# A hybrid decoder block on one core: squares of the last token tile, a later norm, earlier loads for down, and the last sums

## The chip, the core and the metric

The kernel runs on one core of a Trainium2 chip. Its time is the device time of one execution in microseconds (us). The core has five engines with a queue of instructions each: TensorE (PE, with its weight loads PEld), VectorE (DVE), ScalarE (ACT), GpSimd (POOL) and SyncE (SP), which here only issues transfers. Each engine works its queue in order and waits for semaphores of the others.

## What is computed

One layer of a decoder block on 1024 tokens of width 1024: two groups of attention heads in parallel, an output projection, and a gated MLP of inner width 2816. Cut to the parts that the change touches:

```
x = x + concatenate([rmsnorm(nsa, nsa_norm_g), gdn]) @ w_out      # nsa: (tokens, 512)
h = rmsnorm(x, norm2_g)
x = x + (silu(h @ w_gate) * (h @ w_up)) @ w_down
return rmsnorm(x, final_g)

def rmsnorm(x, g):
    y = x * rsqrt(mean(x * x, axis=-1) + 1e-6)
    return y * g
```

## The kernel before

All large products keep fp32 accuracy by three products of a high and a low part: `split3` issues high by high (L119), high by low (L120) and low by high (L121). The parts are made by `split`: ACT writes the high part (a conversion, L1203), and POOL or VectorE subtracts it from the source (L1204). The instructions are written in program order; a scheduler with dependences places them in the queues, and `after(a, b)` holds TensorE's a behind b. Tiles live in rings of slots: a load waits until its slot's last reader is done.

Features lie on partitions and tokens along the free axis. Tokens go in two halves of 512, and features in tiles of 128 (dt 0 to 7).

*Norm of the sparse attention.* Per token tile i of 128 (NT of them), `nsa_square` (L1080) squares the attention output on ACT, and POOL adds its four feature tiles in two steps (L1083, L1084). `nsa_mean` (L1087) sums over partitions on TensorE with a column of ones (L1089); the tile's rows are then scaled (L1104), split into `mgt` (L1110 ACT, L1111) and multiplied by `w_out`.

*Second norm.* As each tile dt of the new x is there (L1176), `sumsq` squares it and adds it to `sqa` (L1195; for the last two of the second half on VectorE). `rnorm_sum` sums `sqa` over partitions on TensorE (L1212), VectorE scales it (L1215) and POOL takes the power -1/2 (L1216). `rnorm_out` spreads the result over partitions on TensorE (L1223). `normed` (L1361) multiplies x by it on VectorE, and `bsplit` (L1366) splits the result.

*MLP, up and gate.* Each of 22 blocks (256 columns of the gate for an even number, of the up for an odd one) is computed in Strassen's manner: products of 12 matmuls of operands A (weights, `Weights`, L1320) and B or T (activations). Block 0 is written out: `prod2` issues two products into one PSUM bank, 24 matmuls, and after step k of 8 (three matmuls each) calls what `between[k]` names. The first, `c11`, uses the first token half alone; the second half's norm is put between its matmuls, since its squares come last. Blocks 1 and 2 have two such products each. Then the loop over blocks (L1452) makes the seven-product sums on VectorE (L1466 to L1475), Silu for the gate on ACT (L1478), the gating product on POOL (L1481), and stores the gated tile in DRAM (`aD`, L1482), as SBUF doesn't hold all of them.

*Down.* `Pair(p)` (L1516) loads the weights of two inner tiles of 128 rows (`draw`, L1495, into the slots "wq" of the weights before) and their gated activations (`bact`, L1501, from `aD` into the ring of 20 slots); there are 11 pairs. Pair 0 is done as plain products (`lead`), pairs 1 to 9 in Strassen's manner, the last as plain products again (`trail`). `Plain` (L1541) splits the four weight tiles on VectorE and the four activation tiles on POOL. Slots for split tiles are handed out by `atile` (6 slots "A", 4 "wk").

*The end.* `trail` makes the last sum of x (L1634) for tokens 0 to 511, then 512 to 767, then 768 to 1023. ACT squares each tile (L1636), POOL adds dt 1 to 7, or 1 to 5 in the last part (L1640); `norm_sum` (L1608) sums over partitions (L1613), VectorE scales (L1616), POOL takes the power (L1617), `norm_out` spreads it (L1623). `scaled` (L1602) of the part before runs between, and stores to `out` (L1606); the last part's scaling is at L1658 to L1665.

## Time and profile before

| | before |
|---|---|
| median of 3 runs | 1481.53 us (1479.89 to 1483.02) |
| the profiled execution | 1479.02 us |
| its span in the profile | 1477.3 us |
| mean granted clock of TensorE | 0.990 |
| PE busy | 96% |
| PEld / DVE / ACT / POOL busy | 81% / 65% / 49% / 48% |
| chain that ended last | PE 61%, DVE 9%, issue 5%, POOL 5%, ACT 4%, DMA 3% |

The profile is of one execution, in us from the start of the span; about 1.7 us of the execution's time lie outside it. A row of the timeline names the start, the duration, the engine, the line of the kernel, the operation with output and input tiles, and how many in a row are drawn together; in brackets stands the idle time of the engine before it and what ended it. Matmuls overlap in the array, so one's duration is longer than the distance to the next. PEclk is the granted clock of TensorE as a share of 2.4 GHz; 0.50 is 1.2 GHz. The MLP's up and gate part runs from about 804 to 1240, down from there to 1465.

### The profile page before, as it was taken

How to read it: one execution, taken by the hardware profiler on the slowest of the kernel's cores; microseconds unless marked ns; L12 is line 12 of the kernel's file. 1: busy time of each engine (PE TensorE's matmuls, PEld its weight loads, DVE VectorE, ACT ScalarE, POOL GpSimd, SP SyncE). 2: the span in 40 equal slices, each digit the busy share in tenths (PEclk: the TensorE clock that was granted, in tenths of full speed). 3: DMA queues.
4: the chain of work that ended last, by engine and by line, in shares of the span. 5: the costliest groups of instructions: out<-in, count | busy, mean ns of one | idle time of the engine just before them, and what ended most of it. 6: DMA issues, size and time to landing. Idle time of an engine off the chain costs nothing.

```text
span 1477.3 us, 22838 instructions
## 1 busy us (share of the span) xinstructions
PE 1417.4 (96%) x7688; PEld 1194.4 (81%) x7688; DVE 965.9 (65%) x2270; ACT 717.6 (49%) x1568; POOL 715.0 (48%) x763
## 2 busy tenths in 40 slices
PE   8999999999998899999999999999999999999997
PEld 8998877999897777777777888888888887888886
DVE  4246688826645899999946954444444444999955
ACT  5433356336556988868754543333333331444423
POOL 1243235651122665654566186665566653345436
PEclk9999999999998999999999999999999999999998
DMA  7832255487536213110155132222222238534003
GB/s 273 275 113 74 96 173 165 115 214 223 160 124 213 82 51 108 50 44 23 43 180 191 29 115 93 83 79 74 79 85 80 86 98 286 190 117 135 1 1 114
DMA packets 142884, 174.92 MB, mean 118 GB/s; under 512 B 26928, under 2 KB 79408, under 8 KB 142640
## 3 DMA queue, kind: packets, MB, share of 16 engines
q1 hardware_dynamic: 142768, 173.47, 37.0%
q8 instruction: 61, 1.00, 0.3%
q14 instruction: 55, 0.45, 0.1%
HBM read 122.01 MB, written 51.41 MB: 117 GB/s over the span
## 4 chain that ended last, share of the span: by engine, by line
PE 61%; DVE 9%; issue 5%; POOL 5%; ACT 4%; DMA 3%; SPq 0%; POOLq 0%; DVEq 0%; ACTq 0%
PE mm L121 16%; PE mm L119 16%; PE mm L120 16%; PE c L1051 3%; PE b L1062 2%; DVE PT L1065 2%; PE a L1012 2%; PE a L650 1%; DVE cy L353 1%; ACT Ps L1029 1%; ACT PT L1064 1%; PE a L657 1%; POOL sqa L1640 1%; DMA mgt<-mgD 1%; PE a L964 1%
## 5 line engine op out<-in xcount | busy, mean ns | idle before, releaser
L1204 POOL TENSOR_TENSOR A<-wq,A 128x512 fp32r<-128x512 f32 x94 | 125.9, 1341 | 95.1 <-ACT A L1203 78.0
L1203 ACT ACTIVATE A<-wq 128x512 fp32r<-128x512 f32 x96 | 60.2, 631 | 134.4 <-PE mm L121 117.1
L119 PE MATMUL mm<-w,xh 128*128 128x256 f32 x384 | 110.6, 288 | 2.5 <-ACT kst L593 2.3
L120 PE MATMUL mm<-w,xh 128*128 128x256 f32 x384 | 110.0, 286 | 2.5 <-POOL w L208 2.5
L1065 DVE TENSOR_TENSOR PT<-b,PT 128x512 fp32r<-128x512 f32 (+1 forms) x148 | 100.9, 685 | 17.4 <-ACT PT L1064 16.6
L121 PE MATMUL mm<-w,xl 128*128 128x256 f32 x384 | 109.8, 286 | 0.0
L1204 POOL TENSOR_TENSOR wk<-wq,wk 128x512 fp32r<-128x512 f32 x61 | 82.4, 1352 | 55.2 <-ACT wk L1203 47.0
L1064 ACT ACTIVATE PT<-b 128x512 fp32r<-128x512 f32 (+1 forms) x148 | 86.1, 589 | 29.4 <-PE b L1062 27.7
L208 POOL TENSOR_TENSOR w<-wraw,w 128x512 fp32r<-128x512 f32 x48 | 64.0, 1353 | 57.7 <-ACT w L205 57.7
L1051 PE MATMUL c<-PT,vs 128*128 128x512 f32 x264 | 90.8, 430 | 0.1
L1203 ACT ACTIVATE wk<-wq 128x512 fp32r<-128x512 f32 x63 | 39.6, 630 | 87.7 <-PE mm L121 80.8
L119 PE MATMUL mm<-T,A 128*128 128x512 f32 x200 | 79.1, 396 | 0.0
L120 PE MATMUL mm<-T,A 128*128 128x512 f32 x200 | 79.1, 396 | 0.0
L121 PE MATMUL mm<-T,A 128*128 128x512 f32 x200 | 79.1, 396 | 0.0
L1481 POOL TENSOR_TENSOR ring<-ring,ring 128x512 f32<-128x512 f32 x44 | 58.4, 1327 | 38.9 <-DVE ring L1466 26.5
L119 PE MATMUL mm<-xh,w 128*128 128x512 f32 x192 | 76.0, 396 | 0.7 <-DVE kcl L417 0.7
L120 PEld LDWEIGHTS mm<-w,xh 128*128 128x128 f32 x384 | 73.5, 191 | 3.4 <-POOL w L208 3.3
L119 PEld LDWEIGHTS mm<-w,xh 128*128 128x128 f32 x384 | 73.5, 191 | 3.1 <-ACT kst L593 2.5
L121 PE MATMUL mm<-xh,w 128*128 128x512 f32 x192 | 75.3, 392 | 0.0
L120 PE MATMUL mm<-xl,w 128*128 128x512 f32 x192 | 74.8, 390 | 0.0
L1513 DVE TENSOR_TENSOR B<-B,mm 128x512 f32<-128x512 f32 x100 | 63.6, 678 | 16.1 <-PE mm L121 15.6
L121 PEld LDWEIGHTS mm<-w,xl 128*128 128x128 f32 x384 | 73.5, 191 | 0.1
(472 smaller groups left out, 4485.5 us busy)
## 6 DMA issues: line engine op xcount, KB each, us to landing
wq<-in_w_gu SPq DMA_DIRECT2D x92, 256.0 KB, 2.7
aD<-ring SPq DMA_DIRECT2D x44, 256.0 KB, 2.2
ring<-aD SPq DMA_DIRECT2D x44, 256.0 KB, 4.4
raw<-in_w_dn SPq DMA_DIRECT2D x36, 256.0 KB, 4.0
qk<-gD SPq DMA_DIRECT2D x16, 512.0 KB, 4.6
wraw<-in_w_out SPq DMA_DIRECT2D x28, 256.0 KB, 2.9
wraw<-in_w_tok SPq DMA_DIRECT2D x24, 256.0 KB, 2.9
wraw<-in_w_gdn SPq DMA_DIRECT2D x24, 256.0 KB, 2.9
```

Of the source, the lines that this page charges most:

```text
L119: after(mm(ps, lhsT=lh, rhs=rh, start=first, stop=False, skip_group_check=grow), prev)
L120: mm(ps, lhsT=lh, rhs=rl, start=False, stop=False, skip_group_check=grow)
L121: return mm(ps, lhsT=ll, rhs=rh, start=False, stop=last, skip_group_check=grow)
L208: (lo or G).tensor_tensor(out=wt[:, 1, k0:k0 + n, :], in0=raw, in1=f32(wt[:, 0, k0:k0 + n, :]), op=ALU.subtract)
L1012: mm(s1[:, 0:a1 - a0], lhsT=QS[:, h, :], rhs=KSs[a][:, g, a0:a1], start=(a == 0), stop=(a == 1))
L1051: mm(po, lhsT=v, rhs=PT[0:K, a], start=(n_ == 0 and a == 0), stop=(n_ == len(blocks) - 1 and a == 1))
L1064: act(out=PT[0:K, 0], in_=pt[0:K], func=AF.Copy)
L1065: V.tensor_tensor(out=PT[0:K, 1], in0=pt[0:K], in1=f32(PT[0:K, 0]), op=ALU.subtract)
L1203: act(out=dst[:, 0], in_=src, func=AF.Copy)
L1204: after(eng.tensor_tensor(out=dst[:, 1], in0=src, in1=f32(dst[:, 0]), op=ALU.subtract), prev)
L1481: G.tensor_tensor(out=t, in0=half[o], in1=t, op=ALU.mult)
L1513: V.tensor_tensor(out=out_, in0=a_, in1=b_, op=op)
```

## The change

It has four parts.

- A: for the last token tile the two POOL adds of the squares go, and `nsa_mean` sums the four parts in TensorE with four matmuls of 2 columns.
- B: in block 0 the sum of the second half's squares moves from behind step 2 of the first product to behind step 5, and the spreading of the norm from behind step 6 to behind step 1 of the second product `c21`.
- C: `draw`, `bact`, `lin` and `Pair` stand ahead of the block loop, and `Pair(0, True)` is made in the last block (b == NF - 1) behind `W.second()`, ahead of its products, instead of in `Plain`; so it is handed to `lead`.
- D: in the last part of the tokens, dt 4 and 5 too go to TensorE instead of POOL; the sums over partitions are ordered by part, with a PSUM bank for each 128 tokens; two VectorE operations scale them. The last scaled part is stored in four transfers of two tiles instead of two of four, by turns from SP's and from ACT's queue.

```
@@ -1080 @@ def nsa_square(i):
         act(out=sq, in_=mn[:, :, i * P:(i + 1) * P], func=AF.Square)
+        if i == NT - 1:
+            return sq
         G.tensor_tensor(out=sq[:, 0:2], in0=sq[:, 0:2], in1=sq[:, 2:4], op=ALU.add)
...
     def nsa_mean(i, sq, bank, tag, prev=None):
         pt = bank(tag)
-        after(mm(pt[:, 0:2], lhsT=sq[:, 0], rhs=ones[:, 0:2], start=True, stop=True), prev)
+        n = 4 if i == NT - 1 else 1
+        for k in range(n):
+            after(mm(pt[:, 0:2], lhsT=sq[:, k], rhs=ones[:, 0:2], start=k == 0, stop=k == n - 1), prev)
@@ -1407 @@
-    c11 = prod2(W.A11, B11, W.A12, B21, {2: norm1_sum, 6: norm1_out})
-    c21 = prod2(W.A21, B11, W.A22, B21)
+    c11 = prod2(W.A11, B11, W.A12, B21, {5: norm1_sum})
+    c21 = prod2(W.A21, B11, W.A22, B21, {1: norm1_out})
@@ -1459 @@ the loop over blocks
             W = wts.pop(b)
             W.second()
+            if b == NF - 1:
+                raws0 = Pair(0, True)
             p1, p2 = P12.pop(b) if b in P12 else (prod(W.A11, B11)[0], prod(W.A12, B21)[0])
@@ -1541 @@ class Plain:
-        def __init__(self, p, engs):
+        def __init__(self, p, engs, raws=None):
             self.fs = [2 * p, 2 * p + 1]
-            raws = Pair(p, True)
+            raws = raws or Pair(p, True)
...
-    lead = Plain(0, (V, G))
+    lead = Plain(0, (V, G), raws0)
@@ -1608 @@
-    def norm_sum(parts, w, prev=None):
+    def norm_sum(parts, w, prev=None, pss=None):
         n = w // P
-        ps = mk(pps4, [P, 512], "n", F32, 2)
-        for j in range(n):
-            for q_, t in enumerate(parts):
-                after(mm(ps[:, 2 * j:2 * j + 2], lhsT=t[:, j * P:(j + 1) * P], rhs=ones[:, 0:2], start=q_ == 0,
+        ps = pss[0] if pss else mk(pps4, [P, 512], "n", F32, 2)
+        for q_, t in enumerate(parts):
+            for j in range(n):
+                o_ = pss[j][:, 0:2] if pss else ps[:, 2 * j:2 * j + 2]
+                after(mm(o_, lhsT=t[:, j * P:(j + 1) * P], rhs=ones[:, 0:2], start=q_ == 0,
                          stop=q_ == len(parts) - 1), prev)
         ms = mk(pc, [P, 2, 4], "ms4", F32, 2)
-        V.tensor_scalar(ms[:, 0, 0:n], ps[:, 0:2 * n:2], 1.0 / D, EPS, op0=ALU.mult, op1=ALU.add)
+        if pss:
+            for j in range(n):
+                V.tensor_scalar(ms[:, 0, j:j + 1], pss[j][:, 0:1], 1.0 / D, EPS, op0=ALU.mult, op1=ALU.add)
+        else:
+            V.tensor_scalar(ms[:, 0, 0:n], ps[:, 0:2 * n:2], 1.0 / D, EPS, op0=ALU.mult, op1=ALU.add)
...
-            if dt >= 6 and o:
+            if dt >= 4 and o:
                 parts.append(s_[:, :w])
...
-    ms = norm_sum(parts, w)
+    ms = norm_sum(parts, w, None, [mk(pps4, [P, 512], "mm", F32, 6) for _ in range(w // P)])
...
-        if dt % 4 == 3:
-            dma(out[:, dt - 3:dt + 1, hf * 512 + o:hf * 512 + o + w], x2[hf][:, dt - 3:dt + 1, o:o + w])
+        if dt % 2:
+            (dma if dt % 4 == 1 else nc.scalar.dma_start)(
+                out[:, dt - 1:dt + 1, hf * 512 + o:hf * 512 + o + w], x2[hf][:, dt - 1:dt + 1, o:o + w])
```

In the changed kernel the lines from L1083 on have other numbers: L1212 is L1216 there, L1223 is L1227, L1204 is L1208, L1481 is L1531, L1482 is L1532, draw's load L1498 is L1451, bact's L1503 is L1456, L1489 is L1539.

TensorE in block 0, around the sum of the second half's squares (`sqa`); A and wk are the split weights, B_1766 the first and B_1767 the second feature half of the activations. Before:

```order
L119 MATMUL mm_9517<-B_1766_9288,A_9332 128x512
L120 MATMUL mm_9517<-B_1766_9288,A_9332 128x512 [waits DVE_49]
L121 MATMUL mm_9517<-B_1766_9288,A_9332 128x512
L1212 MATMUL mm_9527<-ones_81,sqa_9229 128x2 [waits DVE_49]
L1212 MATMUL mm_9527<-ones_81,sqa_9229 128x2 x3
L119 MATMUL mm_9517<-B_1766_9288,A_9332 128x512
L120 MATMUL mm_9517<-B_1766_9288,A_9332 128x512
```
Changed:

```order
L119 MATMUL mm_9518<-B_1767_9290,wk_9336 128x512 [waits Activation_49]
L120 MATMUL mm_9518<-B_1767_9290,wk_9336 128x512 [waits DVE_49]
L121 MATMUL mm_9518<-B_1767_9290,wk_9336 128x512
L1216 MATMUL mm_9537<-ones_81,sqa_9230 128x2 [waits DVE_49]
L1216 MATMUL mm_9537<-ones_81,sqa_9230 128x2 x3
L119 MATMUL mm_9518<-B_1767_9290,wk_9336 128x512 [waits Activation_49]
L120 MATMUL mm_9518<-B_1767_9290,wk_9336 128x512
```
The sum stands behind three steps of the second operand pair now; 12 matmuls lie between it and the spreading of the norm before and after.

SP's queue at the last gating: loads of weights for down (wq from `in_w_dn`), loads of the residual (B from `x3D`), stores of gated tiles (to `aD`) and loads of gated tiles (from `aD`). Before:

```order
L1498 DMA wq_12734<-in_w_dn 128x512
L1498 DMA wq_14348<-in_w_dn 128x512
L1498 DMA wq_14350<-in_w_dn 128x512
L1498 DMA wq_14352<-in_w_dn 128x512
L1489 DMA B_2319_12722<-x3D_68 128x4x512 x2
L1482 DMA aD_69<-ring_12635 128x512
L1489 DMA B_2320_12723<-x3D_68 128x4x512 x2
L1482 DMA aD_69<-ring_12679 128x512
L1503 DMA ring_12736<-aD_69 128x512
L1482 DMA aD_69<-ring_12651 128x512
L1503 DMA ring_12738<-aD_69 128x512
L1503 DMA ring_12740<-aD_69 128x512
```
Changed:

```order
L1451 DMA wq_12614<-in_w_dn 128x512
L1451 DMA wq_14349<-in_w_dn 128x512
L1456 DMA ring_12616<-aD_69 128x512
L1456 DMA ring_12618<-aD_69 128x512
L1456 DMA ring_12620<-aD_69 128x512
L1456 DMA ring_12622<-aD_69 128x512
L1451 DMA wq_14351<-in_w_dn 128x512
L1451 DMA wq_14353<-in_w_dn 128x512
L1539 DMA B_2328_12740<-x3D_68 128x4x512 x2
L1532 DMA aD_69<-ring_12653 128x512
L1539 DMA B_2329_12741<-x3D_68 128x4x512 x2
L1532 DMA aD_69<-ring_12697 128x512
```
The first four loads of gated tiles move from behind two of the last four stores and the residual to directly behind the first five weight loads.

POOL at the same place: gating products (L1481, changed: L1531) and splits of the first pair's activations (from a ring tile by L1204, changed: L1208). Before:

```order
L1204 TENSOR_TENSOR A_12604<-wq_12575,A_12604 128x512
L1481 TENSOR_TENSOR ring_12635<-ring_12494,ring_12635 128x512
L1481 TENSOR_TENSOR ring_12679<-ring_12538,ring_12679 128x512
L1481 TENSOR_TENSOR ring_12651<-ring_12510,ring_12651 128x512
L1481 TENSOR_TENSOR ring_12633<-ring_12492,ring_12633 128x512
L1204 TENSOR_TENSOR wk_12751<-ring_12736,wk_12751 128x512
L1204 TENSOR_TENSOR A_12754<-ring_12740,A_12754 128x512
L1204 TENSOR_TENSOR A_12763<-ring_12738,A_12763 128x512
L1204 TENSOR_TENSOR wk_12766<-ring_12742,wk_12766 128x512
```
Changed:

```order
L1208 TENSOR_TENSOR A_12605<-wq_12576,A_12605 128x512
L1208 TENSOR_TENSOR wk_12752<-ring_12616,wk_12752 128x512
L1208 TENSOR_TENSOR A_12755<-ring_12620,A_12755 128x512
L1531 TENSOR_TENSOR ring_12653<-ring_12495,ring_12653 128x512
L1208 TENSOR_TENSOR A_12764<-ring_12618,A_12764 128x512
L1208 TENSOR_TENSOR wk_12767<-ring_12622,wk_12767 128x512
L1531 TENSOR_TENSOR ring_12697<-ring_12539,ring_12697 128x512
L1531 TENSOR_TENSOR ring_12669<-ring_12511,ring_12669 128x512
L1531 TENSOR_TENSOR ring_12651<-ring_12493,ring_12651 128x512
```
Two of the four splits move ahead of the last four gating products, and two behind the first of them.

## Rows read from the trace of the kernel before

**Rows 1.** the page: busy us (share of the span) and instructions of each engine
```profile
PE 1417.4 (96%) x7688; PEld 1194.4 (81%) x7688; DVE 965.9 (65%) x2270; ACT 717.6 (49%) x1568; POOL 715.0 (48%) x763
```

**Rows 2.** the timeline of TensorE, 770: start us, us, engine line op, [idle before]
```profile
770.13 0.38 PE L1089 MATMUL mm<-ones,wx 128*128 128x2 f32 x2 [1.41 <-POOL wx L1084]
```

**Rows 3.** the timeline of TensorE, first product of the MLP
```profile
803.90 0.39 PE L119 MATMUL mm<-B,A 128*128 128x512 f32 x1
...
805.73 0.39 PE L121 MATMUL mm<-B,A 128*128 128x512 f32 x1
807.61 1.05 PE L1212 MATMUL mm<-ones,sqa 128*128 128x2 f32 x8 [1.50 <-DVE sqa L1195]
...
812.94 1.06 PE L1223 MATMUL mm<-cst,ms 128*128 128x128 f32 x8
...
815.69 0.40 PE L121 MATMUL mm<-B,A 128*128 128x512 f32 x1
```

**Rows 4.** the timeline of VectorE and GpSimd in the same stretch
```profile
806.87 0.68 DVE L1195 TENSOR_TENSOR sqa<-sqa,wx 128x512 f32<-128x512 f32 x1
...
808.94 1.39 POOL L1216 TENSOR_TENSOR ms<-ms,cst 128x4 f32<-128x4 f32 x1 [5.81 <-DVE ms L1215]
...
814.04 2.06 DVE L1361 SCALAR_TENSOR_TENSOR ring<-ring,vec,mm 128x512 f32<-128x512 f32 x3 [4.58 <-PE mm L1223]
```

**Rows 5.** busy us, PE PEld DVE ACT POOL; PEclk, DMA share, GB/s
```profile
809.00:812.00 3.00, 3.00 (x9) 2.32 (x8) 0.46 (x1) 0.00 (x0) 3.00 (x3) 0.50 0.00 0
```

**Rows 6.** the timeline of TensorE, last gating to down
```profile
1239.59 0.40 PE L121 MATMUL mm<-B,A 128*128 128x512 f32 x1
1241.70 0.98 PE L119 MATMUL mm<-wk,wk 128*128 128x512 f32 x3 [1.72 <-ACT wk L1203]
...
1248.42 0.39 PE L119 MATMUL mm<-wk,A 128*128 128x512 f32 x1
```

**Rows 7.** the timeline of SP's queue and ACT, same place
```profile
1239.74 1.40 SPq L1503 DMA_DIRECT2D ring<-aD  x3
...
1241.02 0.63 ACT L1203 ACTIVATE wk<-ring 128x512 fp32r<-128x512 f32 x1 [17.12 <-DMA ring<-aD]
```

**Rows 8.** the timeline at the end, and one stretch's busy times
```profile
1465.82 0.38 PE L1613 MATMUL n<-ones,sqa 128*128 128x2 f32 x2 [0.72 <-POOL sqa L1640]
...
1466.06 0.40 ACT L1636 ACTIVATE gu<-B 128x256 f32<-128x256 f32 x1
...
1467.67 0.16 DVE L1616 TENSOR_SCALAR ms<-n 128x2 f32<-128x2 f32 x1 [1.06 <-PE n L1613]
...
1472.00:1474.00 2.00, 0.00 (x0) 0.00 (x0) 0.40 (x2) 0.00 (x0) 0.49 (x1) 0.50 1.03 335
```

**Rows 9.** the timeline of TensorE, the sums over the first token half
```profile
783.69 0.28 PE L1212 MATMUL mm<-ones,sqa 128*128 128x2 f32 x2
...
786.29 0.48 PE L119 MATMUL mm<-mgt,wk 128*128 128x512 f32 x1
```

**Rows 10.** the timeline at 775, and line 1111's group: ns min/median/max
```profile
775.84 3.94 DVE L1111 TENSOR_TENSOR mgt<-mn,mgt 128x128 fp32r<-128x128 f32 x4 [0.71 <-ACT mgt L1110]
...
777.05 0.50 PE L120 MATMUL mm<-mgt,wk 128*128 128x512 f32 x1 [0.46 <-DVE mgt L1111]
...
L1111 DVE TENSOR_TENSOR mgt<-mn,mgt x4: 279/1262/1369, 775.8 to 779.5; 128x128 fp32r<-128x128 f32 x4
```

**Rows 11.** the timeline of GpSimd and TensorE in block 2
```profile
853.38 2.54 POOL L1204 TENSOR_TENSOR wk<-wq,wk 128x512 fp32r<-128x512 f32 x2
...
856.42 0.40 PE L121 MATMUL mm<-T,wk 128*128 128x512 f32 x1
```

**Rows 12.** SP's queue and VectorE around the last gating, and a stretch
```profile
1206.33 13.18 SPq L1498 DMA_DIRECT2D wq<-in_w_dn  x6
...
1242.20 1.70 DVE L1204 TENSOR_TENSOR wk<-wq,wk 128x512 fp32r<-128x512 f32 x1 [1.49 <-ACT wk L1203]
...
1260.00:1280.00 20.00, 20.00 (x89) 16.39 (x88) 20.00 (x30) 6.57 (x12) 6.52 (x4) 1.00 0.45 167
```

More of the change, by code (lines that the diff above doesn't have):

```diff
@@ L1439, in hybrid_block, with draw, bact, lin @@
         bsplit(T4, k, h0b, V)
+    NRAW, NAB = 16, 8
+    def draw(src, early):
+        r = flat(mk(praw, [P, 4, P], "wq", F32, RAWB)) if early else mk(pm, [P, 512], "raw", F32, NRAW)
+        if src is not None:
+            dma(r, src)
+        return r
+    def bact(f, hf):
+        r = ring()
+        dma(r, aD[f, hf])
+        return r
+    def lin(out_, a_, b_, op):
+        V.tensor_tensor(out=out_, in0=a_, in1=b_, op=op)
+        return out_
+    ADD, SUB = ALU.add, ALU.subtract
+    class Pair:
+        def __init__(self, p, early):
+            self.early = early
+            self.a = {(d, c): draw(w_dn[:, 2 * p + c, d * 512:(d + 1) * 512], early) for c in range(2) for d in range(2)}
+            self.b = {(c, h): bact(2 * p + c, h) for c in range(2) for h in range(2)}
+            self.s1 = draw(None, early)
+        def operands(self, m):
+            a, b = self.a, self.b
+            if m == 1:
+                return a[0, 0], b[0, 0]
+            if m == 5:
+                return lin(self.s1, a[1, 0], a[1, 1], ADD), lin(b[0, 0], b[0, 1], b[0, 0], SUB)
+            if m == 6:
+                lin(a[1, 0], a[0, 0], a[1, 0], SUB)
+                return lin(a[0, 0], self.s1, a[0, 0], SUB), lin(b[0, 0], b[1, 1], b[0, 0], SUB)
+            if m == 3:
+                return lin(self.s1, a[0, 1], a[0, 0], SUB), b[1, 1]
+            if m == 7:
+                return a[1, 0], lin(b[0, 1], b[1, 1], b[0, 1], SUB)
+            if m == 2:
+                return a[0, 1], b[1, 0]
+            return a[1, 1], lin(b[1, 0], b[1, 0], b[0, 0], SUB)
     half = {}
@@ L1489, in hybrid_block @@
             dma(x2[hf][:, 4 * a:4 * a + 4], x3D[hf, 4 * a:4 * a + 4].rearrange("k p t -> p k t"))
-    def draw(src, early):
-        r = flat(mk(praw, [P, 4, P], "wq", F32, RAWB)) if early else mk(pm, [P, 512], "raw", F32, NRAW)
-        if src is not None:
-            dma(r, src)
-        return r
-    def bact(f, hf):
-        r = ring()
-        dma(r, aD[f, hf])
-        return r
     def dsplit(src, eng, early=False):
```

27 lines of the change are left out of this document (removed).

## The prediction

> **What bounds the kernel now.** I read the busy shares of the page first: TensorE works 1417.4 us of a span of 1477.3 [rows 1], so only time in which TensorE stands still, or runs at its lower clock, can be won. I therefore went through TensorE's rows of the timeline for idle time in front of them, and looked for those of the four places that the change touches. They lie in different stages, and each is read there.
>
> - Last token tile's norm: TensorE is idle 1.41 us until the second of two POOL adds of the squares (L1083, L1084) ends [rows 2].
> - First product of the MLP: it starts at 803.90 and keeps 0.229 us per product matmul (eight steps to 805.73). The sum of squares could then start at 805.96 and starts at 807.61, since VectorE ends its last add only at 806.87 + 0.68 = 807.55 [rows 3, 4]. Behind that wait the granted clock is 0.50, the 1.2 GHz level, from 809 to 812 [rows 5].
> - First product of down: the last gating matmul starts at 1239.59, the next could follow at 1239.82, and comes at 1241.70; there ACT's conversion of a tile waited 17.12 us for its load [rows 6, 7].
> - The end: TensorE waits 0.72 us for POOL's last add of squares; then the transfers run at a DMA share of 1.03 [rows 8].
>
> The span is 1477.3 and the execution 1479.02. The sums are made against 1479.02; the median of the runs, 1481.53, is 2.5 above it, and I carry the same difference over.
>
> **A, the last token tile's squares.** Two POOL adds go, and TensorE sums four parts: 8 instructions instead of 2. Such instructions were issued 24 in 786.29 - 783.69 = 2.60 us, 0.108 each [rows 9], so six more cost 0.65. TensorE wins 1.41 - 0.65 = 0.76 there. What is late next is the first product with this tile. Its ACT conversion (L1110, at 775.51) stands behind another conversion that a load feeds, and doesn't move; VectorE's four subtractions behind it take 3.94 us in all, and TensorE waits for three of them, 0.46 at the first [rows 10]; the others are 0.33 and 0.34. The shortest of the four takes 0.28, the median is 1.26 [rows 10], and in the timeline each long one ends as a POOL split ends. POOL loses 1.19 us of adds (0.74 and 0.45), but its next splits hang on ACT's conversions, and I find it only some 0.15 earlier. So nearly all is given back: **0.2 us**, between 0.1 and 0.76.
>
> The Trainium skill (GPSIMD Engine Reference, section Specifications) says that GpSimd's memory interfaces are shared with VectorE, with contention where a VectorE instruction has two SBUF inputs. The rows above show that stretch; without such a rule the subtractions would take 0.28 each and A would be worth 0.7.
>
> **B, the second half's norm.** The sum goes from behind 9 matmuls to behind 18, the broadcast from behind 21 to behind 30; nothing is added. The 30th matmul's slot ended at 815.69 + 0.23 = 815.92. A small group costs its 1.05 or 1.06 less the 0.39 - 0.229 = 0.16 that matmuls overlap, so 0.89 and 0.90. With no wait and the full clock the same point comes at 803.90 + 30 x 0.229 + 0.89 + 0.90 = 812.56. That is **3.36 us**: 1.65 of waiting, and the 12 matmuls between sum and broadcast, which took 812.94 - 808.50 = 4.44 instead of 2.75, 1.69 [rows 3]. The cover: TensorE reaches the sum at 803.90 + 18 x 0.229 = 808.02, and VectorE is done at 807.55, a margin of 0.47. From the sum's end to the end of POOL's power it took 808.94 + 1.39 - 808.50 = 1.83 [rows 4], so the power is there at 808.91 + 1.83 = 810.74, and TensorE asks for it at 808.91 + 12 x 0.229 = 811.66. The operands of the nine matmuls that now come sooner were written before 804.4 (VectorE's adds of squares at 804.35 and 806.87 stand behind them).
>
> But the second half's normalization on VectorE hangs on the broadcast: it starts 1.10 behind it, at 814.04 [rows 4], and will start at 811.66 + 1.10 = 812.76, only 1.28 earlier, where TensorE is 3.36 earlier. The chain of VectorE, ACT and POOL that feeds the products loses 2.08 us of its lead. From 815 to 1239 TensorE has no idle time in the timeline; the smallest lead that I find is in block 2: POOL ends a split at 853.38 + 2.54 / 2 = 854.65, and TensorE wants it at 856.42 [rows 11], a lead of 1.77. It becomes -0.3, and with A's gain -0.5. So I take 3.36 - 0.5 = **2.8 us**; the bounds are 3.4 (nothing given back) and 1.6 (the chain isn't earlier at all, and the lead of 1.77 less A's gain is all there is).
>
> Of the granted clock the windows show 1.00 (2.4 GHz) up to 808 and 0.50 (1.2 GHz) from 809 to 812, after 1.65 us without a product and 0.89 of small matmuls. The wait of 1.41 of [rows 2] was followed by no such fall, nor were the 24 small matmuls of [rows 9] that had no wait ahead. With the wait gone I take the full clock. The Trainium skill (TensorE: Matmul & The Clock Gate, section HAM oscillation) says that a wait between bursts of matmuls is paid a second time, in throttled matmuls behind it. By it the 1.69 goes with the wait, as I take it; if the small group alone were the cause, 1.69 would stay.
>
> **C, the first pair of down.** Its four weight loads and four loads of activations are now asked for ahead of the last gating. In SP's queue the weights stand where they stood; four loads of activations go past two weight loads, the four loads of the residual and the stores of the last gated tiles, behind which they stood (1239.74 for three of them [rows 7]). The queue gives out that stretch's weight loads between 1206.33 and 1219.51 [rows 12], so the activations are asked for by 1220 at the latest and there by 1224 (the page's median for such a load is 4.4). The slots of their split tiles come free with the products of the last gating, by 1234.3 as I count them at 12 x 0.23 = 2.8 us for a product, so all eight splits can be done by about 1236, before TensorE wants them at 1239.82. TensorE needed until 1248.42 for the 24 matmuls that follow; from 1241.70 that is 6.72 against 24 x 0.229 = 5.50. Won: 1.88 + 1.22 = 3.10.
>
> What moves with them: one ACT conversion of an early activation now stands ahead of the last Silu and of the last gating's copy; of POOL's four splits two stand ahead of the last gating's four multiplications and two behind the first, whose stores so come up to 1 us later; these are read only at the end of down, so that costs nothing. Two splits of VectorE go from 1242 to before 1240, where VectorE waits for TensorE anyway; this cover matters, as VectorE is busy 20.00 of 20 us in 1260 to 1280 [rows 12] and must be 3 us earlier there. The two splits (1.70 [rows 12], and 1.42 for the other) give it just that. I take **3.0 us**, and 1.5 as the low end (half is given back by a VectorE that stays late).
>
> **D, the end.** Sums of dt 4 and 5 go from POOL to TensorE: 20 small instructions instead of 12, 8 x 0.108 = 0.86 more, that start with the last product at about 1465.1 instead of 1465.82. Sixteen take until 1466.8; the last four need ACT's square, done at 1466.06 + 0.40 [rows 8]; so TensorE is done at about 1467.3, and VectorE, which read the sums at 1467.67 [rows 8], can at 1467.4. It then has two short operations of 0.16 instead of one. The mean is there some 0.1 to 0.3 earlier. But the transfers take the DMA engines whole from 1470 to 1475.8 (share 1.03 in 1472 to 1474), and the finer outputs, half of them from ACT's queue, don't change the bytes. **0.1 us**, between -0.5 (no row shows a transfer from ACT's queue; two SP issues took 1.21) and 0.6. The Trainium skill (DMA: Bandwidth & Descriptors, section Rules for kernel authors) says that issuing from several engines doesn't help bandwidth and saves issue time alone. Going by that sentence D gets no more than 0.6, and the share of 1.03 agrees.
>
> **Sum:** 0.2 + 2.8 + 3.0 + 0.1 = 6.1. Execution 1472.9, median 1481.53 - 6.1 = **1475.4 us**.
>
> **Rivals.** *1. The feeders give most back.* Lead lost by B and a full VectorE in down keep TensorE waiting in block after block; B falls to 1.0 and C to 1.5: 2.5 in all, 1479.0. For it: VectorE at 20.00 of 20; against: the leads of the other blocks, 5 to 10 us. *2. The sum still waits or the clock falls anyway.* The margin is 0.47; if VectorE's add is 0.5 later, or the small group alone brings a clock of 0.50, B keeps 1.65 less the 0.5 given back: 1.15 and 3.3 from the rest, 4.45, so 1477.1. Against: the 24 small ones of [rows 9]. *3. Slower: ACT is blocked.* ACT works in order, and a conversion of the early activations now stands ahead of its last Silu and the copy of the last gating's product. If that load lands after 1232 instead of 1224, the copy, VectorE's adds and with them the PSUM banks stop, and TensorE stands until the load is there: as late as the old 1241.7, that is 9.7 us of waiting, less the 3.1 of C (down then follows without a wait) and the 3.1 of A, B and D: 3.5 us slower, 1485.0. It decides from the load's landing at 1232; against it stands the queue's last issue at 1219.5, 12 us before. *4. The loads stay where they were* (the pair's tiles come free too late): then C is 0 and the time 1478.4. The order of SP's queue speaks against it.
>
> **How the numbers follow.** Forecast 0.70, rival 1 0.12, rival 2 0.10, rival 3 0.05, rival 4 0.03. A measurement of this kernel can tell 0.2%, 3 us, from no change. Faster by more: forecast, rivals 2 and 4, 0.83; within: rival 1, 0.12; slower: rival 3, 0.05. The range: all highs are 0.76 + 3.4 + 3.1 + 0.6 = 7.9, which gives 1473.6, and 1.6 below for the runs' own spread (1479.89 against 1481.53), 1472.0; the upper end takes in rival 1 with some of that spread, 1480.0.
>
> **What would show it.** A: the idle 1.41 ahead of the tile's sum gone, the waits of the next tile's products longer by some 0.5. B: no wait ahead of the sum of squares, granted clock 1.00 throughout 803 to 816, the broadcast near 811.5, and a wait of under 1 us near 853. C: no idle time between the last gating and down, four loads asked for before 1220. D: the last sums ended by 0.3 sooner and a DMA share of 1 to the end. The forecast is wrong if a wait of over 1 us on ACT or VectorE appears in the last gating or in 1260 to 1320, or the clock shows 0.50 in the first products.

## The result

The changed kernel took 1475.04 us in the median (9 runs, 1471.59 to 1480.48) against 1482.14 before (9 runs). The ratio is 0.9949, with a 95% interval of 0.9936 to 0.9962: 7.6 us faster, between 5.6 and 9.5. 1475.4 was forecast. Timed again later, the same kernel stood at 0.9944 (0.9930 to 0.9958).

The page of the changed kernel: span, busy times and the chain that ended last.

```profile
span 1472.9 us, 22871 instructions
PE 1416.7 (96%) x7702; PEld 1196.2 (81%) x7702; DVE 963.6 (65%) x2271; ACT 717.6 (49%) x1568; POOL 723.9 (49%) x759
PE 62%; DVE 9%; issue 6%; POOL 4%; ACT 4%; DMA 2%; SPq 0%; DVEq 0%; POOLq 0%; ACTq 0%
```

TensorE's busy time is within 0.7 us of what it was [rows 1: 1417.4]; the span is 4.4 us shorter. That is less than the times say, and a span alone can't be read here. Up to 765 us both kernels issue the same instructions, and yet that stretch ended at 764.9 before and at 766.1 after; among the 14 traces of this study it ended between 764.9 and 768.3. So I compare stage by stage: I count the product matmuls (L119 to L121) back from the last one, and take the time between fixed ones. Both kernels have the same number of them.

| stage, by its start in the trace of before | before | after | difference |
|---|---|---|---|
| last token tile, 764.89 to 780.66 | 15.77 | 15.34 | -0.43 |
| second half's output products, to 802.75 | 22.09 | 21.95 | -0.14 |
| first products of the MLP, to 817.06 | 14.31 | 11.44 | -2.87 |
| blocks, to 1233.98 | 416.92 | 416.94 | 0.02 |
| last gating and first pair of down, to 1250.91 | 16.93 | 13.80 | -3.13 |
| down, to 1429.65 | 178.74 | 178.73 | -0.01 |
| down's end, to 1450.02 | 20.37 | 19.93 | -0.44 |
| last products, to 1464.82 | 14.80 | 16.55 | 1.75 |
| from the last product to the end of the span | 12.49 | 12.13 | -0.36 |

The sum is -5.61, after the last products gave 1.75 back. (The last row takes the spans to 0.01 us, 1477.31 and 1472.85.) The places, one after the other.

TensorE in the last token tile's stage (start us, us, engine, line, operation; in brackets the idle time before it and what ended it):

```profile
769.72 1.01 PE L1093 MATMUL mm<-ones,wx 128*128 128x2 f32 x8
...
776.91 0.51 PE L119 MATMUL mm<-mgt,wk 128*128 128x512 f32 x1 [0.32 <-ACT mgt L1114]
777.77 0.50 PE L120 MATMUL mm<-mgt,wk 128*128 128x512 f32 x1 [0.36 <-DVE mgt L1115]
```

The idle 1.41 of [rows 2] is gone, and eight small instructions stand in its place. But the first product with this tile now waits 0.32 for ACT's conversion, and the waits for VectorE's subtractions are still there, 0.36 for 0.46 [rows 10].

TensorE, VectorE and GpSimd (POOL) in the timeline around the first products:

```profile
804.48 0.39 PE L119 MATMUL mm<-B,A 128*128 128x512 f32 x1
...
808.99 1.05 PE L1216 MATMUL mm<-ones,sqa 128*128 128x2 f32 x8 [0.24 <-DVE sqa L1199]
...
812.74 1.05 PE L1227 MATMUL mm<-cst,ms 128*128 128x128 f32 x8
...
797.75 3.08 DVE L1370 TENSOR_TENSOR B<-ring,B 128x512 fp32r<-128x512 f32 x2
...
798.90 1.38 POOL L1199 TENSOR_TENSOR sqa<-sqa,wx 128x512 f32<-128x512 f32 x1 [0.33 <-ACT wx L1195]
...
808.25 0.69 DVE L1199 TENSOR_TENSOR sqa<-sqa,wx 128x512 f32<-128x512 f32 x1
...
813.83 2.07 DVE L1365 SCALAR_TENSOR_TENSOR ring<-ring,vec,mm 128x512 f32<-128x512 f32 x3 [3.49 <-PE mm L1227]
```

The busy times of a stretch there (PE, PEld, DVE, ACT, POOL; then the granted clock, DMA share, GB/s):

```profile
809.00:812.00 3.00, 3.00 (x17) 2.66 (x18) 1.30 (x3) 0.63 (x1) 1.58 (x2) 1.00 0.00 0
```

The clock is 1.00 where [rows 5] had 0.50. The sum still waits 0.24: VectorE ends its last add at 808.94, not 807.55 [rows 4], and TensorE comes at 808.59. Two splits of VectorE at 797.75 took 3.08 us where the same two took 1.97 before:

```profile
797.02 1.97 DVE L1366 TENSOR_TENSOR B<-ring,B 128x512 fp32r<-128x512 f32 x2
...
798.47 1.68 POOL L1195 TENSOR_TENSOR sqa<-sqa,wx 128x512 f32<-128x512 f32 x1 [0.62 <-ACT wx L1191]
```

The difference lies in the second of the two, 0.68 us before (from 798.32) and 1.78 after (from 799.05), and it goes with who starts first. Before, this split started 0.15 us ahead of GpSimd's addition of squares (798.47), and the addition took 1.68. After, it started 0.15 behind that addition (798.90), which took 1.38. All fourteen traces of this study go one way or the other: 0.68 us and ahead in the seven without part A, 1.78 us and behind in the seven with it. The normalization behind the broadcast starts at 813.83, only 0.21 earlier than in [rows 4].

POOL's split and TensorE's first use of its low part in block 2:

```profile
852.69 1.29 POOL L1208 TENSOR_TENSOR wk<-wq,wk 128x512 fp32r<-128x512 f32 x1
...
854.16 0.40 PE L121 MATMUL mm<-T,wk 128*128 128x512 f32 x1
```

The split ends at 853.98 and is wanted at 854.16: the lead was 1.77 [rows 11] and is 0.18, and TensorE doesn't wait.

SP's queue, POOL and TensorE at the last gating, and the stretch of [rows 12]:

```profile
1212.36 1.85 SPq L1456 DMA_DIRECT2D ring<-aD  x4
...
1232.91 1.29 POOL L1208 TENSOR_TENSOR wk<-ring,wk 128x512 fp32r<-128x512 f32 x1 [1.51 <-ACT wk L1207]
...
1237.32 0.40 PE L121 MATMUL mm<-B,A 128*128 128x512 f32 x1
1237.56 0.39 PE L119 MATMUL mm<-wk,wk 128*128 128x512 f32 x1
```

The busy times of a stretch there (PE, PEld, DVE, ACT, POOL; then the granted clock, DMA share, GB/s):

```profile
1260.00:1280.00 20.00, 20.00 (x89) 16.33 (x88) 20.00 (x31) 8.91 (x16) 8.40 (x5) 1.00 0.30 102
```

The four loads are asked for from 1212.36, the last split is done at 1234.20, and down's first product follows the gating at the distance of matmuls, 0.24. VectorE is still busy 20.00 of 20 us and holds nobody up.

TensorE at the first sum over partitions of the last products, and the clock behind it:

```profile
1446.96 1.05 PE L1622 MATMUL n<-ones,sqa 128*128 128x2 f32 x8 [1.06 <-POOL sqa L1653]
```

The same sum in the trace of before:

```profile
1452.55 1.05 PE L1613 MATMUL n<-ones,sqa 128*128 128x2 f32 x8 [0.81 <-POOL sqa L1640]
```

The busy times of a stretch behind it in the changed kernel (PE, PEld, DVE, ACT, POOL; then the granted clock, DMA share, GB/s):

```profile
1448.00:1450.00 2.00, 2.00 (x12) 2.00 (x12) 0.58 (x2) 0.28 (x1) 1.71 (x2) 0.57 0.00 0
```

This wait was 0.81 before, with a clock of 1.00 throughout; it is 1.06 here, and the clock fell to 0.57 in the mean of 1448 to 1450. That is the 1.75 given back.

The end: TensorE's small matmuls, VectorE's two scalings, the spreading, and the last transfers by SP and ACT:

```profile
1460.85 0.50 PE L1622 MATMUL mm<-ones,sqa 128*128 128x2 f32 x4
...
1463.02 0.31 DVE L1627 TENSOR_SCALAR ms<-mm 128x1 f32<-128x1 f32 x2 [0.50 <-PE mm L1622]
...
1464.17 0.71 PE L1636 MATMUL n<-cst,ms 128*128 128x128 f32 x4 [1.03 <-POOL ms L1630]
...
1466.49 1.22 SPq L1678 DMA_DIRECT2D out<-B  x2
1466.94 1.16 ACTq L1678 DMA_DIRECT2D out<-B  x2
```

The busy times of a stretch there (PE, PEld, DVE, ACT, POOL; then the granted clock, DMA share, GB/s):

```profile
1469.00:1471.00 2.00, 0.00 (x0) 0.00 (x0) 0.00 (x0) 0.00 (x0) 0.00 (x0) 0.50 1.04 344
```

From the last product matmul the sums are read 2.3 us later (1460.73 to 1463.02) instead of 2.9 (1464.82 to 1467.67, [rows 8]); the transfers run at a share of 1.04 up to the end, as before.

### The profile page after: what moved, and what is told of

It is laid out like the page before. It is cut to its first block, busy times and chain, and to the rows that moved or that the text cites. A ratio compares the mean times of both kernels' runs of the same rounds, so it can differ in the third digit from the quotient of the medians.

```text
span 1472.9 us, 22871 instructions
## 1 busy us (share of the span) xinstructions
PE 1416.7 (96%) x7702; PEld 1196.2 (81%) x7702; DVE 963.6 (65%) x2271; ACT 717.6 (49%) x1568; POOL 723.9 (49%) x759
## 4 chain that ended last, share of the span: by engine, by line
PE 62%; DVE 9%; issue 6%; POOL 4%; ACT 4%; DMA 2%; SPq 0%; DVEq 0%; POOLq 0%; ACTq 0%
PE mm L119 17%; PE mm L121 17%; PE mm L120 17%; PE c L1051 3%; PE b L1062 2%; DVE PT L1065 2%; PE a L1012 2%; PE a L650 1%; DVE cy L353 1%; ACT Ps L1029 1%; ACT PT L1064 1%; PE a L657 1%; DMA mgt<-mgD 1%; POOL sqa L1653 1%; PE a L964 1%
## 5 line engine op out<-in xcount | busy, mean ns | idle before, releaser
L1208 POOL TENSOR_TENSOR A<-wq,A 128x512 fp32r<-128x512 f32 x94 | 141.4, 1507 | 94.9 <-ACT A L1207 83.6
L119 PE MATMUL mm<-w,xh 128*128 128x256 f32 x384 | 111.2, 290 | 2.6 <-ACT kst L593 2.6
L121 PE MATMUL mm<-w,xl 128*128 128x256 f32 x384 | 110.5, 288 | 0.0
L1208 POOL TENSOR_TENSOR wk<-wq,wk 128x512 fp32r<-128x512 f32 x61 | 82.5, 1353 | 49.5 <-ACT wk L1207 44.8
L119 PE MATMUL mm<-T,A 128*128 128x512 f32 x200 | 79.1, 396 | 0.0
L121 PE MATMUL mm<-T,A 128*128 128x512 f32 x200 | 79.1, 396 | 0.0
L119 PEld LDWEIGHTS mm<-w,xh 128*128 128x128 f32 x384 | 74.2, 193 | 2.9 <-ACT kst L593 2.8
L119 PE MATMUL mm<-xh,w 128*128 128x512 f32 x192 | 75.9, 395 | 0.7 <-DVE kcl L417 0.7
L121 PE MATMUL mm<-xh,w 128*128 128x512 f32 x192 | 75.3, 392 | 0.0
L121 PEld LDWEIGHTS mm<-w,xl 128*128 128x128 f32 x384 | 74.3, 193 | 0.1
L353 DVE SCALAR_TENSOR_TENSOR cy<-cr,vec,cy 128x512 f32<-128x512 f32 x72 | 62.4, 867 | 17.1 <-ACT cy L351 7.3
```

The source lines that it names most:

```text
L119: after(mm(ps, lhsT=lh, rhs=rh, start=first, stop=False, skip_group_check=grow), prev)
L121: return mm(ps, lhsT=ll, rhs=rh, start=False, stop=last, skip_group_check=grow)
L353: V.scalar_tensor_tensor(out=y, in0=cr[:, j:j + 512], scalar=cw[:, j:j + 1], in1=y, op0=ALU.mult, op1=ALU.add)
L1208: after(eng.tensor_tensor(out=dst[:, 1], in0=src, in1=f32(dst[:, 0]), op=ALU.subtract), prev)
```

## The experiments

**Each part alone.** Four kernels, each the kernel before with one part of the change.

Part A:

```
+        if i == NT - 1:
+            return sq
...
-        after(mm(pt[:, 0:2], lhsT=sq[:, 0], rhs=ones[:, 0:2], start=True, stop=True), prev)
+        n = 4 if i == NT - 1 else 1
+        for k in range(n):
+            after(mm(pt[:, 0:2], lhsT=sq[:, k], rhs=ones[:, 0:2], start=k == 0, stop=k == n - 1), prev)
```

> Part A alone. By the ledger of the two traces A wins 0.95 us where the idle time ahead of the tile's sum was, and gives 0.5 back where VectorE's four subtractions end with POOL's splits: 0.4 us faster in all, ratio 0.9997, not to be told from 1 in the times, but plain in the trace as the distance from the last product before the sum to the first product of the second token half at 803.90. Rival: nothing holds those subtractions but their source, then the full 0.75 to 0.95 stays. Other rival: the first use of the tile hangs on loads and everything is given back, 0.

Measured: 1485.24 us, ratio 1.0022 (1.0011 to 1.0034): 3.3 us slower. TensorE at the tile's first product and at the sum of the second half's squares, and ACT's conversion ahead of the tile's:

```profile
777.71 0.50 PE L119 MATMUL mm<-mgt,wk 128*128 128x512 f32 x1 [1.10 <-ACT mgt L1114]
...
809.65 1.05 PE L1216 MATMUL mm<-ones,sqa 128*128 128x2 f32 x8 [2.21 <-DVE sqa L1199]
...
775.00 0.63 ACT L1207 ACTIVATE A<-wq 128x512 fp32r<-128x512 f32 x1 [1.75 <-DMA wq<-in_w_gu]
```

The 0.95 us won at the tile's sum (2.05 us from the product ahead of it to the one behind it became 1.10) are lost at once: the tile's conversion stands behind one that waited 1.75 us for its load, and TensorE waits 1.10 for it; the stage takes 15.94 us, 0.17 more than before. Then the sum of squares waits 2.21 instead of 1.50, and the first products take 15.06 instead of 14.31. None of the three had foreseen a loss. The traces account for 0.9 us of it, and 0.3 more in the first pair of down; 2 us of the 3.3 by the times are not seen in this one trace, which is that of the fastest of twelve runs (1481.41 us). Over the twelve, the mean granted clock was 0.987, against 0.989 in this trace and 0.988 over the 62 runs of the kernel before; so time at the lower clock is a likely place for the rest, not a shown one.

Part B:

```
-    c11 = prod2(W.A11, B11, W.A12, B21, {2: norm1_sum, 6: norm1_out})
-    c21 = prod2(W.A21, B11, W.A22, B21)
+    c11 = prod2(W.A11, B11, W.A12, B21, {5: norm1_sum})
+    c21 = prod2(W.A21, B11, W.A22, B21, {1: norm1_out})
```

> Part B alone. Theory: the wait ahead of the sum and the low clock behind it go together; 2.8 to 3.4 us, ratio 0.9977 to 0.9981, granted clock 1.00 from 804 to 816, and at most 0.4 us of idle time ahead of the sum. Rival 1: the group of eight small matmuls brings the clock down by itself; then 0.50 shows again behind it and 1.2 to 1.7 us are won, ratio 0.9989. Rival 2: the lead of the feeders in block 2 (1.77 us before) is used up: a wait of 0.3 to 1.0 us shows near 853, and 2.3 are won.

Measured: 1479.25 us, ratio 0.9981 (0.9969 to 0.9993). TensorE at the sum of squares (no idle time in front), then at the first pair of down, and the clock there:

```profile
810.03 0.95 PE L1212 MATMUL mm<-ones,sqa 128*128 128x2 f32 x8
...
1240.06 0.97 PE L119 MATMUL mm<-wk,wk 128*128 128x512 f32 x3 [1.41 <-ACT wk L1203]
1242.53 0.79 PE L120 MATMUL mm<-wk,wk 128*128 128x512 f32 x1 [1.50 <-POOL wk L1204]
```

The busy times of a stretch there (PE, PEld, DVE, ACT, POOL; then the granted clock, DMA share, GB/s):

```profile
1244.00:1246.00 2.00, 2.00 (x6) 1.61 (x5) 0.55 (x1) 0.69 (x2) 2.00 (x2) 0.50 0.92 330
```

The first products take 10.94 us for 14.31: 3.37 won, with no wait at the sum and none in block 2 (416.93). Both rivals fall. What wasn't expected stands at the first pair of down, which this kernel doesn't touch: behind a wait of 1.41 the clock falls to 0.50 at about 1241.3, a second wait of 1.50 comes while it is low, and the stage takes 19.92 us, 3.0 more than in the trace of before, where waits of 1.72 and 0.73 left the clock at 1.00.

Part C:

```
...
+            if b == NF - 1:
+                raws0 = Pair(0, True)
...
-    lead = Plain(0, (V, G))
+    lead = Plain(0, (V, G), raws0)
```

> Part C alone. Theory: TensorE goes from the last gating into down without idle time, 3.1 us, ratio 0.9979, and keeps them to the first sum of the last products. Rival: VectorE, full from 1260 to 1280, can't be 3 us earlier; then waits on it show between 1250 and 1330 and about 1.5 are left, ratio 0.999. In the last stage the trace of the changed kernel lost 1.6 us behind the first sum over partitions (1447): if that comes from TensorE being earlier than POOL's adds, it shows here as well (a wait over 1 us and a clock under 1.00 there); if it differs from execution to execution, some of these four traces have it and others not, whatever part they hold.

Measured: 1478.32 us, ratio 0.9973 (0.9962 to 0.9983): 4.0 us, between 2.5 and 5.6. The stage takes 13.79 us for 16.93, so 3.14 in this trace; down behind it takes 178.74 as before, so VectorE held nobody up and the rival falls. That the times give more than 3.1 agrees with the stage's two sizes without this part: 16.93 and 17.27 (before, A alone) where the clock stayed, 19.92 and 19.86 (B alone, D alone) where it fell. In the ten traces with this part the stage took 13.79 or 13.80. The wait in the last products was 0.81 here, at a clock of 1.00: not part C alone makes it longer.

Part D:

```
...
-            if dt >= 6 and o:
+            if dt >= 4 and o:
...
+            (dma if dt % 4 == 1 else nc.scalar.dma_start)(
```

> Part D alone. Theory: the end from the last product to the end of the span is 12.05 us as in the changed kernel, against 12.36 before; 0.3 us, ratio 0.9998, not to be told from 1 in the times. Rival 1: the transfers alone set the end, 0. Rival 2: the first transfers issued by ACT start late, 0.5 us slower.

Measured: 1482.60 us, ratio 0.9998 (0.9987 to 1.0009). The end took 12.14 us against 12.49; over all traces it is 12.12 to 12.17 with this part (ten) and 12.48 to 12.50 without (four). So the theory holds by the traces, and the times can't tell it.

**Variants of the changed kernel.** Four kernels, timed together.

Without part A (its lines above taken out again):

> The changed kernel without part A (B, C and D). Part A alone was 0.22% slower, so the question is whether it costs in the changed kernel too. Theory: alone, A let TensorE come to the sum of the second half's squares earlier and VectorE later, and the wait there grew from 1.50 to 2.21 us; behind B that wait is 0.24, so A is worth between +0.4 and -0.4 us here, and this kernel is like the changed one: ratio to before 0.9945 to 0.9955. Rival: A's own cost (0.2%, 3 us) is independent of B; then this kernel is about 1472 us, ratio 0.993.

Measured: 1472.12 us, ratio 0.9931 (0.9918 to 0.9943). By the stages, the tile takes 15.77 as before, and the first products 10.94, where the changed kernel takes 11.44. So A wins 0.43 in one stage and costs 0.50 in the next. The last products take 14.79 for 16.55; that is not A's own work, since two kernels with A (the next one and the one on GpSimd) take 14.80 there. The time is the rival's, 1472 us, 0.18% under that of the changed kernel; but the changed kernel was timed on another occasion, and the two were timed side by side below.

The sum one step later:

```
-    c11 = prod2(W.A11, B11, W.A12, B21, {5: norm1_sum})
-    c21 = prod2(W.A21, B11, W.A22, B21, {1: norm1_out})
+    c11 = prod2(W.A11, B11, W.A12, B21, {6: norm1_sum})
+    c21 = prod2(W.A21, B11, W.A22, B21, {2: norm1_out})
```

> The changed kernel with the sum of the second half's squares one step of three matmuls later still (behind 21 instead of 18, and the broadcast behind 33). Theory: the wait left there, 0.24 us idle and 0.4 in the distance of the matmuls, goes: 0.4 us, not to be told in the times; the later broadcast takes 0.3 us of the feeders' lead, which was 0.18 in block 2, so up to 0.5 us comes back as a wait near 852. Rival: leads as small as 0.18 are already waits in disguise, then nothing shows at 852.

Measured: 1477.71 us, ratio 0.9962 (0.9949 to 0.9975). TensorE and POOL in block 2, and the clock behind:

```profile
858.90 0.50 PE L121 MATMUL mm<-T,wk 128*128 128x512 f32 x1 [2.68 <-POOL wk L1208]
...
856.36 1.27 POOL L1531 TENSOR_TENSOR ring<-ring,ring 128x512 f32<-128x512 f32 x1
857.59 2.50 POOL L1208 TENSOR_TENSOR wk<-wq,wk 128x512 fp32r<-128x512 f32 x2
```

The busy times of a stretch there (PE, PEld, DVE, ACT, POOL; then the granted clock, DMA share, GB/s):

```profile
860.00:862.00 2.00, 2.00 (x6) 1.55 (x5) 0.00 (x0) 0.00 (x0) 2.00 (x3) 0.50 0.67 182
```

The wait at the sum is gone (first products 10.94), and at the very place that the prediction named TensorE waits 2.68 us for POOL's split, with a clock of 0.50 behind it: the blocks take 421.42 for 416.94. It is more than the 0.5 expected, since the order of the queues changed too. Counted from the first product, the broadcast came 0.17 us later than in the changed kernel, but the split 2.46: VectorE's steps ahead of it came 1.27 later, in another order, and a gating product of POOL (856.36) now stands ahead of the split. The lead of 0.18 in the changed kernel is no wait, and a smaller one is, as the theory had it; but the 4.5 us are the price of this step with the order that the scheduler gave it, and not that of a shorter lead alone.

Two additions in the last products on VectorE:

```
-                G.tensor_tensor(out=sq[:, :w], in0=sq[:, :w], in1=s_[:, :w], op=ALU.add)
+                (V if dt >= 6 and not hf else G).tensor_tensor(out=sq[:, :w], in0=sq[:, :w], in1=s_[:, :w], op=ALU.add)
```

> The changed kernel with the last two additions of squares of the first part of the last products (dt 6 and 7, 512 tokens) on VectorE instead of GpSimd. Theory: the wait of 1.06 us ahead of the first sum there (0.80 to 0.81 in the other kernels) goes, and with it the chance of the low clock behind it, which cost 1.6 us in one trace of six: 0.8 to 1.1 us, ratio to the changed kernel 0.9993. Rival: VectorE's additions come late as well, or delay its sums of x, and the wait stays with VectorE as its end.

Measured: 1470.36 us, ratio 0.9917 (0.9904 to 0.9930). TensorE's first sum there, without idle time in front:

```profile
1447.14 1.02 PE L1622 MATMUL n<-ones,sqa 128*128 128x2 f32 x8
```

The last products take 13.79 us, against 14.80 where the wait is 0.80 and 16.55 where the clock falls behind it: the theory holds by the trace. The ratio is 0.32% under that of the changed kernel, more than four times what the theory gave; it was measured again below.

The low parts of the last token tile on GpSimd:

```
-    nsa_split(ms1, NT - 1, 1, V)
+    nsa_split(ms1, NT - 1, 1, G)
```

> The changed kernel with the low parts of the last token tile made by GpSimd instead of VectorE (four operations of 128 by 128). It asks what holds VectorE's four subtractions for 3.5 to 3.9 us. Theory: they share the way to memory with GpSimd's splits; in GpSimd's own queue they take some 0.4 us each (a 128 by 128 addition took 0.45), so TensorE's three waits of 0.32 to 0.36 there shrink, and the first product of the second half comes about 0.5 us earlier. Rival: they stand behind GpSimd's splits in its queue, and TensorE waits as long or longer, up to 3 us more.

Measured: 1476.82 us, ratio 0.9964 (0.9953 to 0.9976).

```profile
779.65 0.50 PE L120 MATMUL mm<-mgt,wk 128*128 128x512 f32 x1 [1.87 <-POOL mgt L1115]
```

The busy times of a stretch there (PE, PEld, DVE, ACT, POOL; then the granted clock, DMA share, GB/s):

```profile
780.00:782.00 2.00, 2.00 (x7) 1.63 (x6) 0.00 (x0) 0.56 (x1) 2.00 (x4) 0.62 0.89 310
```

One wait of 1.87 us takes the place of three of a third each, a lower clock follows, and the stage takes 17.13 for 15.34. The clock is low a second time from 790.7, and the output products take 23.76 for 21.95. The rival was right: behind GpSimd's splits in its own queue the subtractions come later still. What holds them on VectorE is not settled by this kernel.

**The four side by side.** The changed kernel, it without A, it with the two additions on VectorE, and both at once, timed together.

> The changed kernel once more, beside the next three on the same chip, since its ratio to before (0.9949) and those of its versions (0.9931 and 0.9917) are from different calls. Theory: 0.9945 to 0.9952 again. Rival: it lies with its versions, at 0.993, and the difference of 0.2% between them was one of calls.

> The changed kernel without part A, again. Theory (A costs about 0.2% wherever it stands, by unsteady loads at 775 and a later VectorE ahead of the sum at 808): 0.15 to 0.2% under the changed kernel of this call. Rival (the ledger of the single traces, in which A with B is worth 0.2 us either way): within 0.1% of it.

> The changed kernel with two additions of squares on VectorE in the last stage, again. Theory: 1.0 us by the wait and some more by a clock that no longer falls behind it in part of the executions: 0.07 to 0.15% under the changed kernel. Rival: 0.3% as between the calls, which would need a clock that falls there in most executions (1.6 us each).

> Both at once: the changed kernel without A and with the two additions on VectorE. Theory: the two savings lie in different stages and add up, 0.2 to 0.35% under the changed kernel, ratio to before about 0.992: the fastest of all. Rival: A costs nothing, then it is as fast as the version with A and the two additions.

| kernel | ratio to before | 95% interval | tile | output products | first products | last products |
|---|---|---|---|---|---|---|
| changed | 0.9944 | 0.9930 to 0.9958 | 15.22 | 21.98 | 11.42 | 16.56 |
| without A | 0.9937 | 0.9923 to 0.9951 | 15.77 | 22.04 | 10.93 | 14.81 |
| with the two additions | 0.9940 | 0.9928 to 0.9952 | 15.74 | 21.96 | 11.44 | 13.78 |
| both | 0.9942 | 0.9929 to 0.9954 | 15.77 | 23.61 | 10.97 | 13.78 |

The times don't tell the four apart: the 0.2 and 0.3% seen between separate timings did not come back. The changed kernel came out as its theory said (0.9944 for 0.9945 to 0.9952). For A the rival holds (0.07% under the changed kernel); the additions give 0.04%, less than the theory and far less than its rival; both together 0.02%. The stages do tell them apart, and repeat: without A the first products are 0.49 shorter, with the additions the last are shorter by 1.0 or 2.8. In the trace of the last kernel the clock is low for a time in the output products, which no part touches, and that costs 1.6 us. It falls at about 789.4, 7 us behind the last of the three waits for the tile's subtractions, so what set it off is not shown (busy times of the stretch; the clock is the last number but two):

```profile
790.00:798.00 8.00, 8.00 (x35) 6.59 (x34) 4.25 (x7) 3.79 (x6) 5.39 (x5) 0.83 0.54 179
```

So no version is shown to beat the changed kernel. By the stages the two additions should be worth 1.0 to 2.8 us, with A or without; a difference of that size is at the edge of what these times can tell.

## Why the prediction was right, and where it was not

The forecast was 6.1 us; the times give 7.6 (5.6 to 9.5) and, timed again, 8.3 (6.2 to 10.4). The stages of the single trace give 5.6.

*A, 0.2 forecast.* The gain at the tile, 0.43, lies in the range given, and most of the 0.95 won at the sum goes back to the tile's conversion and VectorE's subtractions, as forecast. The step that failed stands in B's cover: "VectorE is done at 807.55" was carried over from the trace of before. With A, VectorE was done at 808.94, and the sum waited 0.40 (with the distance of a matmul counted). In five traces with A and B the first products take 11.41 to 11.46 us; in the one with the later sum, and in all four without A, 10.93 to 10.97. So A is worth 0.43 less 0.50 there: nothing, or a little less. In the traces with A the tile's stage itself varies between 15.22 and 15.94 (the variant on GpSimd left out); without A it is 15.76 to 15.78 in seven of seven. TensorE waits 0.3 to 1.1 for the tile's conversion in every trace with A, and in none without. What makes VectorE late is the split near 799: with A, GpSimd's addition starts ahead of it instead of behind it, and in all seven traces with A the last add ends 4.39 to 4.45 us behind the first product, in all seven without 3.65 to 3.70.

*B, 3.36 gross, 2.8 net.* Gross it was 3.37 (B alone, and without A). The clock went back to 1.00 with the wait, and the eight small matmuls alone didn't lower it, in none of ten traces. Of rival 2 the first condition came true with A (VectorE's add was 0.8 us later, counted from the first product), but the wait that it left was 0.40 and brought no low clock, so the 1.15 that it left of B did not come. The 0.5 given back in block 2 didn't come. The place was right, and the lead shrank from 1.77 to 0.18. Counted from the first product's start (0.58 later than before in this trace), TensorE came 2.84 earlier and not 3.36, for the 0.5 that A costs. POOL's split came 1.25 earlier, the number forecast (1.28), but not by the forecast's reason: the broadcast came only 0.8 earlier, for the same 0.5. Without A the broadcast came 1.32 earlier, TensorE 3.36 and the split 1.79, and the lead was 0.20. So the step that failed there is that the chain moves by the broadcast's shift alone: it moved 0.5 us further both times. VectorE and POOL have their instructions in another order between broadcast and split; which of it saves the 0.5 is not shown. That the first products with A gained 2.87, next to the 2.8 forecast net, is luck: the 0.5 was lost at the sum and not in block 2.

*C, 3.0.* 3.13 in the trace, 13.79 or 13.80 in every trace that has it. The mechanism is as forecast, with loads asked for at 1212.36 and the last split at 1234.20 (1220 and 1236 were the latest expected). What I missed is that such waits cost 6.1 us in two of four traces of kernels without C, by the clock behind them. I had read 1.00 there from one trace. This makes C's worth larger than 3.1 in the mean; its own ratio gives 4.0. The untraced runs point the same way: the mean granted clock is 0.9884 over 62 runs of the kernel before, 0.990 in its trace, and 0.990 over 15 runs of the changed kernel. By the difference of 0.0016, some 5 us more at half clock than in the trace, I estimate 2 to 3 us of time, about what the times give beyond the stages' 5.6; where in those runs the clock fell is not shown.

*D, 0.1.* 0.35, in ten traces against four. The sums are read 0.6 earlier, not 0.27 as forecast (1467.4 for 1467.67), and half of that reaches the end.

*Not in the forecast.* Down's end became 0.44 shorter in every trace with B and in none without; there, a wait of 0.19 for VectorE's last but one sum of the pairs (L1513), ahead of the first product of `trail`, was gone. The instructions stand in the same order there with B and without. What removes the wait is not shown. And the last products lost 1.75 in both traces of the changed kernel itself: the wait at the first sum was 1.06 and 1.04 there, with a lower clock behind it, but 0.80 or 0.81 in nine other traces, among them those of three variants whose instructions from the first pair of down on stand in the same order. The delay begins at one instruction, the third of POOL's additions, which starts 0.37 us behind the second (1439.78 to 1440.15) instead of 0.08; the square that it adds was ready at the same distance from a fixed product with this gap and without it:

```profile
1437.06 2.72 POOL L1653 TENSOR_TENSOR sqa<-sqa,gu 128x512 f32<-128x512 f32 x2 [9.07 <-ACT gu L1649]
1440.15 6.76 POOL L1653 TENSOR_TENSOR sqa<-sqa,gu 128x512 f32<-128x512 f32 x5 [0.37 <-POOL sqa L1653]
```

In the variant on GpSimd the same additions follow one another without that gap:

```profile
1440.83 5.47 POOL L1653 TENSOR_TENSOR sqa<-sqa,gu 128x512 f32<-128x512 f32 x4 [9.07 <-ACT gu L1649]
```

The gap stands in all four traces of the changed kernel and of it with the two additions on VectorE, and in none of the ten others. What makes POOL start that instruction late stays open.

The forecast was thus near the truth in part by luck. B's and C's mechanisms hold, with 3.37 and 3.13 us in the stages. Around them stand errors of opposite sign: A's worth (nothing for 0.2), the 0.5 in block 2 that didn't come, down's end (0.44) and the last products (-1.75), which no term named, and the falls of the clock behind waits of about 1 us, of which the change removes two places and meets a third.

## What to carry to other kernels

Before moving a step later in a full queue, find the tightest lead (the time from a tile's completion to its first use) behind it and count it down, and read the new order of the other queues as well: here 3.4 us were had at one step, and 4.5 lost at the next, where VectorE and POOL had another order too. A wait of 1 us or more on TensorE should be priced with and without a fallen clock behind it, since kernels with the same instructions at a place did either there. And compare stages by counting the same matmuls in both traces; the first 765 us alone, the same in all kernels here, differed by up to 3.4 us, more than a part of the change is worth.

## What the runs showed of the hardware

- After waits in front of TensorE the granted clock fell to 0.50 in some executions and not in others. At the first pair of down it fell behind a first wait of 1.41 (B alone) or 1.26 (D alone), and a second wait of 1.50 or 1.64 came while it was low; behind 1.72 and 0.73 (before), or 1.52 and 1.39 (A alone), it stayed at 1.00. A fall there cost 2.6 to 3.0 us. In the last products, behind a wait of 0.80 or 0.81 it never fell (nine traces), behind 1.04 and 1.06 it did both times, and the stage took 1.75 us more. In the output products it fell in two traces out of thirteen (the variant on GpSimd left out), about 7 us behind the last of the three waits for the last token tile, for 1.5 to 1.6 us; no wait stands just ahead of it there.
- VectorE's 128 by 512 subtractions with both inputs in SBUF take 0.6 us each in a row. Beside an addition of GpSimd, the one of the two that started second took longer: a subtraction that started 0.15 us ahead took 0.68 and the addition 1.68 or 1.69 (seven traces); one that started 0.15 us behind took 1.78 and the addition 1.38 (seven traces). The Trainium skill (GPSIMD Engine Reference, section Specifications) says that GpSimd's interfaces to SBUF are shared with VectorE, with contention where a VectorE instruction has two inputs there; the trace agrees. No run took GpSimd's work away, so the sharing is argued from the order of the starts.
- Another issuing engine brought no bandwidth: the DMA share at the end was 1.04 with it and 1.03 without, and 256 KB landed 3.7 us behind the issue from ACT's queue and 3.4 from SP's. The Trainium skill (DMA: Bandwidth & Descriptors, section Issuing engines are not separate DMA queues) says that transfers run on the same DMA engines whichever engine issues them, and the trace agrees. The transfers of the changed kernel's end by issuing queue (KB each, median us from issue to landing):

```profile
out<-B SPq DMA_DIRECT2D x2, 256.0 KB, 3.4
out<-B ACTq DMA_DIRECT2D x2, 256.0 KB, 3.7
```
